# Moving two streamed activation tiles by 16 bytes within their partitions, in a kernel of three transformer layers

## The chip, the cores and the metric

The kernel runs on one core of one Trainium2 chip. The metric is the device time of one execution in microseconds (us); the kernel before has a median of 1132.21 us over 3 runs.

## The reference

Two blocks run one behind the other on 256 tokens of width 1024, all in float32. The first has two layers (a mixer and an MLP with squared ReLU each) and a final norm, the second has one layer. Cut to its core:

```python
for i in range(2):
    hn = rms_norm(x, norm_mix[i])
    mix = even_mixer(hn, ...) if i % 2 == 0 else odd_mixer(hn, ...)
    x = x + mix
    x = x + sqrelu_mlp(rms_norm(x, norm_mlp[i]), mlp_w1[i], mlp_w2[i])
x = rms_norm(x, norm_final)

h = rms_norm_2(x, mix_norm_pre)
xa, ga, q, k, v, f_logit, g_a, g_b = jnp.split(h @ w_in, offs, axis=-1)
y_a = gelu(ga) * rg_lru(causal_dwconv(xa, conv_a_w, conv_a_b), ...)
y_b = forgetting_attention(q, k, v, f_logit + b_forget)
merged = sigmoid(g_a + b_merge[0]) * (y_a @ w_proj_a) + sigmoid(g_b + b_merge[1]) * (y_b @ w_proj_b)
x = x + rms_norm_2(merged @ w_out, mix_norm_post)
h = rms_norm_2(x, ffn_norm_pre)
gate, val = jnp.split(causal_dwconv(h @ w_up, conv_f_w, conv_f_b), 2, axis=-1)
x = x + rms_norm_2((gelu(gate) * val) @ w_down, ffn_norm_post)
```

Here `even_mixer` holds a sparse attention with three branches and a differential attention, `odd_mixer` a block attention. Most of the arithmetic is products with the weight matrices, in float32, each read once.

## The kernel before

The activations lie transposed: 128 partitions hold a slice of the features, the 256 tokens lie along the partition. A tile of width 1024 is `[128, 8, 256]`, eight slices (`KT`, index k) of 256 float32 values, 1024 bytes each.

A float32 product is made of three matmuls of type `float32r`. Each operand is split into a high part and a low part, and `mm3` (lines 279 to 282) adds high x high, high x low and low x high in PSUM. The weights are the stationary operand, the activations the streamed one:

```python
def mm3(o, wh, wl, xh, xl, start, stop, skip=False):
    nc.tensor.matmul(out=o, lhsT=wh, rhs=xh, start=start, stop=False, skip_group_check=skip)
    nc.tensor.matmul(out=o, lhsT=wh, rhs=xl, start=False, stop=False, skip_group_check=skip)
    nc.tensor.matmul(out=o, lhsT=wl, rhs=xh, start=False, stop=stop, skip_group_check=skip)
```

`gh` and `gl` (lines 121 and 122) are the high and the low part of the normed layer input. Nearly all stages that read the residual stream take them as `xh` and `xl`: the projections into the mixers (lines 1168 on, 1290 on, 1512 on), the first matrix of both MLPs (`gen_pair(16, gh, gl, ...)` in `mlp`), the output projection of the second block (line 1635) and its up projection (line 1699). The second matrices of the MLPs stream `hh` and `hl`, the attention outputs `oh` and `ol`, the recurrent branch `yh` and `yl`. ACT and DVE write `gh` and `gl` between the stages (`split`, lines 269 to 277, and lines 1644 and 1648).

Three loops do the streaming with `mm3`: `gen_pair` (two units of weights of 128 columns per PSUM tile, eight k each), `gen_deep` (a matrix with 24 or 32 slices), `gen_half` (four slices at a time). `gen_small` does the same with weights of 24 or 16 columns. In `gen_nat` (lines 453 to 455) and `gen_wide` (lines 475 to 477) the roles are exchanged: the weight matrix is streamed, 256 or 512 columns of it, and a slice of `gh` or `gl` is the stationary operand.

Weights come as chunks of 1 MB into three buffers `raw` by DMA from the SP queue (`w_load`, line 198). `w_parts` splits half a chunk at a time into a unit: ACT copies it into `whi` (line 238), DVE subtracts to get `wlo` (line 239); six buffers of each hold the units for PE, and `w_next` (line 254) keeps three units ahead. The order on every engine is written out by hand (`tc.manual_schedule()`); the pieces of an attention are woven between the matmuls of the projections.

Where a tile lies in its partition is set by the order of the pools and by `pad`, which allocates a filler tile of n float32:

```python
pad(xp, 32)
x = xp.tile([128, KT, T], F32, name="x")
pad(xp, 48)
gh = xp.tile([128, KT, T], FR, name="gh")
gl = xp.tile([128, KT, T], FR, name="gl")
```

The pools stand in the order `cp`, `xp`, `np` (norms: `acc`, `rn`, `rv`, `dg`, `rb`, `sq`, `rb1`), `rawp` (`raw`, `raws`), `wp` (`whi`, `wlo`, behind `pad(wp, 96)` on line 190), and then the pools of the single stages, most of them behind a `pad` of 48. By this the streamed tiles `gh`, `gl`, `hh`, `hl`, `oh`, `ol`, `yh` and `yl` begin 192 bytes behind a multiple of 512, and `whi` and `wlo` at a multiple of 512. Tile starts are given by the pools in steps of 32 bytes.

Of the kernel before, what the change touches and what calls it, by code (L numbers as in the profile page):

```python
# [8 lines left out]
FR = mybir.dt.float32r  # L9
# [5 lines left out]
T = 256  # L15
D = 1024
KT = 8
# [41 lines left out]
def kernel(  # L59
# [30 lines left out]
    xp = ctx.enter_context(tc.tile_pool(name="xp", bufs=1))  # L90
# [3 lines left out]
    def pad(pool, n):  # L94
        pads.append(0)
        pool.tile([128, n], F32, tag="pad%d" % len(pads), name="pad", bufs=1)

    rawp = ctx.enter_context(tc.tile_pool(name="rawp", bufs=3))
    wp = ctx.enter_context(tc.tile_pool(name="wp", bufs=6))
# [18 lines left out]
    pad(xp, 32)  # L118
    x = xp.tile([128, KT, T], F32, name="x")
    pad(xp, 48)  # L120
    gh = xp.tile([128, KT, T], FR, name="gh")
    gl = xp.tile([128, KT, T], FR, name="gl")

    R_CMP, R_ATT0, R_ATT1, R_ATT2 = 2.0, 0.33, 0.7, 1.3

# [61 lines left out]
    add_stream(w_up, U8)  # L187
    add_stream(w_dn, U8)

    pad(wp, 96)  # L190
    W = Ctl()
    W.raw = []
    W.q = []
# [1774 lines left out]
```

## Time and profile before

| | |
|---|---|
| median of 3 runs | 1132.21 us |
| the runs | 1131.8, 1132.21, 1145.28 us |
| the profiled execution: its own time | 1144.74 us |
| its span, first to last instruction | 1143.0 us |
| mean granted TensorE clock | 0.993 |
| busy: PE, PEld, DVE, ACT, POOL | 97%, 93%, 67%, 54%, 18% |
| moved by DMA | 199.98 MB, mean 175 GB/s |

PE is the matrix engine's matmuls, PEld its weight loads (which overlap the matmuls), DVE the vector engine, ACT the scalar engine, POOL GpSimd, SP the engine whose queue issues the weight loads from memory. The profile is one execution; its own time exceeds its span by what lies before the first and behind the last instruction, 1.7 us. Matmuls overlap: the duration of one runs from its start until its last result, so two or three are in flight at a time, and the rate is read from starts or from counts over a stretch. PEclk is the granted clock as a share of 2.4 GHz.

### The profile page before, as it was taken

Reading aid. Unit: us, or ns where it says so; the run is one execution under the profiler, and the core shown is the slowest. Engines: PE = TensorE matmul, PEld = TensorE weight load, DVE = VectorE, ACT = ScalarE, POOL = GpSimd, SP = SyncE. Lnnn points to the kernel's source line nnn. Section 1 sums busy time; section 2 is a strip of 40 time slices with the busy share of each in tenths; the row PEclk is TensorE's granted clock in tenths of the full one; section 3 lists DMA queues with packets and bytes.
Section 4 is the critical chain, followed back from the end, with each engine's and each line's share of the span. In section 5 each row is a group of like instructions: output and inputs, shape, how many; then the busy total and the mean of one; then the engine's idle time right before and its main releaser. Section 6 shows DMA issues by size and latency. Waiting matters only on the chain.

```text
span 1143.0 us, 22253 instructions
## 1 busy us (share of the span) xinstructions
PE 1112.3 (97%) x9151; PEld 1062.5 (93%) x9151; DVE 768.0 (67%) x1355; ACT 615.2 (54%) x1081; POOL 204.4 (18%) x228
## 2 busy tenths in 40 slices
PE   8999899999999999999999999999999989999996
PEld 7987799999999898999999998899899989999996
DVE  5767776665445776666454688866667679988642
ACT  4446555654434555465353486754455557766441
POOL 2014420000010122000011100043310125444211
PEclk9999999999999999999999999999999989999998
DMA  8842243565454333455545454474455535555541
GB/s 329 297 149 74 75 163 139 214 217 197 179 221 177 121 122 146 144 214 185 221 151 227 177 196 147 149 271 140 147 193 174 184 130 171 201 190 188 193 148 37
DMA packets 31301, 199.98 MB, mean 175 GB/s; under 512 B 3594, under 2 KB 6042, under 8 KB 9056
## 3 DMA queue, kind: packets, MB, share of 16 engines
q1 hardware_dynamic: 28832, 187.23, 45.6%
q0 software_dynamic: 2080, 11.08, 2.9%
q8 instruction: 72, 1.18, 0.4%
q10 hardware_dynamic: 288, 0.26, 0.1%
q14 instruction: 29, 0.24, 0.1%
HBM read 197.43 MB, written 3.22 MB: 176 GB/s over the span
## 4 chain that ended last, share of the span: by engine, by line
PE 88%; DVE 5%; ACT 3%; POOL 1%; DMA 1%; issue 1%; SPq 0%; POOLq 0%; ACTq 0%; DVEq 0%
PE g L280 25%; PE g L282 24%; PE g L281 24%; PE rgp L1453 2%; PE pt L660 1%; PE g L475 1%; PE g L477 1%; PE g L476 1%; PE o L710 1%; PE s L616 1%; DVE wlo L239 1%; ACT whi L238 1%; DMA x<-in_xT_dram 1%; PE nsum L342 1%; DMA fb<-scr 1%
## 5 line engine op out<-in xcount | busy, mean ns | idle before, releaser
L239 DVE TENSOR_TENSOR wlo<-raw,whi 128x1024 fp32r<-128x1024 f32 (+2 forms) x356 | 427.8, 1232 | 120.8 <-ACT whi L238 120.5
L280 PE MATMUL g<-gh,whi 128*128 128x256 f32 x1632 | 463.3, 284 | 4.2 <-ACT whi L238 2.7
L281 PE MATMUL g<-gl,whi 128*128 128x256 f32 x1632 | 457.5, 280 | 0.5 <-DVE gl L275 0.4
L282 PE MATMUL g<-gh,wlo 128*128 128x256 f32 x1632 | 457.4, 280 | 0.3
L238 ACT CAST whi<-raw 128x1024 fp32r<-128x1024 f32 (+2 forms) x356 | 349.8, 1024 | 20.4 <-PE g L281 9.7
L280 PEld LDWEIGHTS g<-gh,whi 128*128 128x128 f32 x1632 | 309.7, 190 | 11.6 <-issue 4.8
L281 PEld LDWEIGHTS g<-gl,whi 128*128 128x128 f32 x1632 | 310.7, 190 | 1.2 <-DVE gl L275 0.7
L282 PEld LDWEIGHTS g<-gh,wlo 128*128 128x128 f32 x1632 | 309.9, 190 | 1.1 <-DVE wlo L239 1.1
L280 PE MATMUL g<-hh,whi 128*128 128x256 f32 x704 | 196.6, 279 | 0.0
L282 PE MATMUL g<-hh,wlo 128*128 128x256 f32 x704 | 196.5, 279 | 0.0
L281 PE MATMUL g<-hl,whi 128*128 128x256 f32 x704 | 196.5, 279 | 0.0
L282 PEld LDWEIGHTS g<-hh,wlo 128*128 128x128 f32 x704 | 133.3, 189 | 0.0
L281 PEld LDWEIGHTS g<-hl,whi 128*128 128x128 f32 x704 | 132.9, 189 | 0.0
L280 PEld LDWEIGHTS g<-hh,whi 128*128 128x128 f32 x704 | 132.2, 188 | 0.0
L335 POOL TENSOR_TENSOR acc<-acc,sq 128x256 f32<-128x256 f32 x53 | 42.3, 803 | 464.4 <-ACT sq L331 463.5
L649 POOL TENSOR_TENSOR p<-p,rr 128x384 f32<-128x384 f32 x56 | 50.2, 896 | 199.8 <-DVE rr L644 92.4
L634 ACT ACTIVATE p<-p,nm 128x256 f32<-128x256 f32 x112 | 49.9, 448 | 54.4 <-DVE nm L625 54.2
L280 PE MATMUL g<-oh,whi 128*128 128x256 f32 x192 | 54.9, 286 | 0.0
L1202 ACT ACTIVATE u<-u 128x512 f32<-128x512 f32 x32 | 20.2, 633 | 62.0 <-DVE u L1201 62.0
L281 PE MATMUL g<-ol,whi 128*128 128x256 f32 x192 | 53.5, 278 | 0.0
L282 PE MATMUL g<-oh,wlo 128*128 128x256 f32 x192 | 53.4, 278 | 0.0
L272 DVE TENSOR_TENSOR hl<-u,hh 128x512 fp32r<-128x512 f32 x32 | 22.2, 693 | 43.3 <-ACT hh L271 43.3
(320 smaller groups left out, 1388.5 us busy)
## 6 DMA issues: line engine op xcount, KB each, us to landing
raw<-in_w_in_dram SPq DMA_DIRECT2D x30, 1024.0 KB, 4.9
raw<-in_w_up_dram SPq DMA_DIRECT2D x24, 1024.0 KB, 4.8
raw<-in_w_m1a_dram SPq DMA_DIRECT2D x16, 1024.0 KB, 4.8
raw<-in_w_m2a_dram SPq DMA_DIRECT2D x16, 1024.0 KB, 4.9
raw<-in_w_m1b_dram SPq DMA_DIRECT2D x16, 1024.0 KB, 4.8
raw<-in_w_m2b_dram SPq DMA_DIRECT2D x16, 1024.0 KB, 4.9
raw<-in_w_od_dram SPq DMA_DIRECT2D x12, 1024.0 KB, 5.0
raw<-in_w_dn_dram SPq DMA_DIRECT2D x12, 1024.0 KB, 4.9
```

The costliest lines, as they stand in the source:

```text
L238: nc.scalar.copy(out=hi[:, a:b], in_=t[:, off + a:off + b])
L239: nc.vector.tensor_tensor(out=lo[:, a:b], in0=t[:, off + a:off + b], in1=hi[:, a:b].bitcast(F32), op=ALU.subtract)
L272: nc.vector.tensor_tensor(out=lo, in0=src, in1=hi.bitcast(F32), op=ALU.subtract)
L280: nc.tensor.matmul(out=o, lhsT=wh, rhs=xh, start=start, stop=False, skip_group_check=skip)
L281: nc.tensor.matmul(out=o, lhsT=wh, rhs=xl, start=False, stop=False, skip_group_check=skip)
L282: nc.tensor.matmul(out=o, lhsT=wl, rhs=xh, start=False, stop=stop, skip_group_check=skip)
L335: nc.gpsimd.tensor_tensor(out=self.acc, in0=self.acc, in1=dst, op=ALU.add)
L342: nc.tensor.matmul(out=ps[:, b:b + 1], lhsT=self.parts[i][:, b * 128:b * 128 + 128], rhs=ones[:, 0:1], start=i == 0 and b == 0, stop=i == ...
L634: nc.scalar.activation(out=p[:, c0:c1], in_=p[:, c0:c1], func=AF.Exp, scale=-1.0, bias=nm[:, b:b + 1], accum_out=sm[:, b:b + 1],)
L649: nc.gpsimd.tensor_tensor(out=pv, in0=pv, in1=w, op=ALU.mult)
L1202: nc.scalar.activation(out=u, in_=u, func=AF.Square)
L1453: nc.tensor.matmul(out=ps[c, m, :], lhsT=w[:, m, prs[pi], c], rhs=xc[:, half * 5 + pi, :], start=n == 0, stop=n == len(order) - 1, skip_gr ...
```

## The change

`gh` and `gl` become the two halves of one tile that is 8 float32 longer than both, and begin 4 float32 (16 bytes) into it. The filler before `whi` is made 8 float32 smaller.

```diff
     pad(xp, 48)
-    gh = xp.tile([128, KT, T], FR, name="gh")
-    gl = xp.tile([128, KT, T], FR, name="gl")
+    ghl = xp.tile([128, 2 * KT * T + 8], FR, name="gh")[:, 4:4 + 2 * KT * T].rearrange("p (a k t) -> p a k t", a=2, t=T)
+    gh, gl = ghl[:, 0], ghl[:, 1]
...
-    pad(wp, 96)
+    pad(wp, 88)
```

| tile | start behind a multiple of 512 before, bytes | after |
|---|---|---|
| `gh`, `gl` | 192 | 208 |
| `acc` | 192 | 224 |
| `dg`, `rb`, `sq` | 320 | 352 |
| `raw`, `raws` | 384 | 416 |
| `whi`, `wlo` | 0 | 0 |
| `hh`, `hl`, `oh`, `ol`, `yh`, `yl` | 192 | 192 |

The instructions of each engine, their order and the semaphores and values they wait for are the same in both programs; in the changed one both halves go by the name `gh`.

## Rows read from the trace of the kernel before

**Rows 1.** The page: busy us (share of the span), and the span in 40 slices

```profile
PE 1112.3 (97%) x9151; PEld 1062.5 (93%) x9151; DVE 768.0 (67%) x1355; ACT 615.2 (54%) x1081; POOL 204.4 (18%) x228
...
PE   8999899999999999999999999999999989999996
...
PEclk9999999999999999999999999999999989999998
```

**Rows 2.** The page's costliest groups: busy us, mean ns of one, idle before

```profile
L280 PE MATMUL g<-gh,whi 128*128 128x256 f32 x1632 | 463.3, 284 | 4.2 <-ACT whi L238 2.7
L281 PE MATMUL g<-gl,whi 128*128 128x256 f32 x1632 | 457.5, 280 | 0.5 <-DVE gl L275 0.4
L282 PE MATMUL g<-gh,wlo 128*128 128x256 f32 x1632 | 457.4, 280 | 0.3
```

**Rows 3.** Table of stretches (us): busy and count by engine, clock, DMA share, GB/s

```profile
187.00:242.00 55.00, 55.00 (x488) 55.00 (x487) 38.88 (x43) 31.89 (x41) 0.00 (x0) 1.00 0.55 195
250.00:325.00 75.00, 75.00 (x664) 75.00 (x663) 39.91 (x44) 33.34 (x44) 4.44 (x6) 1.00 0.52 197
473.50:534.00 60.50, 60.50 (x516) 60.50 (x515) 41.72 (x46) 35.34 (x46) 0.00 (x0) 1.00 0.57 200
545.00:620.00 75.00, 75.00 (x639) 75.00 (x638) 34.99 (x39) 32.18 (x47) 8.42 (x12) 1.00 0.50 192
945.00:1056.00 111.00, 111.00 (x944) 111.00 (x944) 102.57 (x146) 77.73 (x125) 50.93 (x43) 1.00 0.54 183
1062.00:1124.00 62.00, 62.00 (x529) 62.00 (x528) 28.01 (x27) 26.66 (x39) 8.51 (x10) 1.00 0.41 146
```

**Rows 4.** Timeline of PE at 182 us: start us, duration us

```profile
182.03 0.28 PE L281 MATMUL g<-gl,whi 128*128 128x256 f32 x1
182.46 0.39 PE L282 MATMUL g<-gh,wlo 128*128 128x256 f32 x1
182.68 0.28 PE L280 MATMUL g<-gh,whi 128*128 128x256 f32 x1
```

**Rows 5.** Timeline of PE at 473 us

```profile
472.73 0.28 PE L281 MATMUL g<-gl,whi 128*128 128x256 f32 x1
473.15 0.38 PE L282 MATMUL g<-gh,wlo 128*128 128x256 f32 x1
473.37 0.28 PE L280 MATMUL g<-gh,whi 128*128 128x256 f32 x1
```

**Rows 6.** Groups of PE by line and shape, 701 to 702.5 us

```profile
L280 PE MATMUL gs<-gh,whi 128*16 128x256 f32 x5 | 1.4, 276 | 0.0
L281 PE MATMUL gs<-gl,whi 128*16 128x256 f32 x5 | 1.4, 276 | 0.0
L282 PE MATMUL gs<-gh,wlo 128*16 128x256 f32 x5 | 1.4, 276 | 0.0
```

**Rows 7.** The same view, gen_nat, 67.5 to 69.5 us, then 70.5 to 72.5 us

```profile
L453 PE MATMUL g<-whi,gh 128*128 128x256 f32 x7 | 1.9, 276 | 0.0
...
L453 PE MATMUL g<-whi,gh 128*128 128x256 f32 x6 | 1.7, 279 | 0.0
```

**Rows 8.** The same view, 187 to 242 us, then 473.5 to 534 us

```profile
L281 PE MATMUL g<-gl,whi 128*128 128x256 f32 x163 | 45.0, 276 | 0.0
...
L281 PE MATMUL g<-gl,whi 128*128 128x256 f32 x172 | 48.3, 281 | 0.0
```

**Rows 9.** The page: splitting of weights on DVE and ACT, and loads of weights

```profile
L239 DVE TENSOR_TENSOR wlo<-raw,whi 128x1024 fp32r<-128x1024 f32 (+2 forms) x356 | 427.8, 1232 | 120.8 <-ACT whi L238 120.5
...
L238 ACT CAST whi<-raw 128x1024 fp32r<-128x1024 f32 (+2 forms) x356 | 349.8, 1024 | 20.4 <-PE g L281 9.7
...
raw<-in_w_in_dram SPq DMA_DIRECT2D x30, 1024.0 KB, 4.9
```

**Rows 10.** The page: the chain that ended last, by line

```profile
PE g L280 25%; PE g L282 24%; PE g L281 24%; PE rgp L1453 2%; PE pt L660 1%; PE g L475 1%; PE g L477 1%; PE g L476 1%; PE o L710 1%; PE s L616 1%; DVE wlo L239 1%; ACT whi L238 1%; DMA x<-in_xT_dram 1%; PE nsum L342 1%; DMA fb<-scr 1%
```

## The prediction

> **What bounds the kernel now.** I read the page's busy shares first, then the costliest groups of instructions, then the table of stretches, and last the timeline at two places where the matrix engine stood still.
>
> The busy shares and the slices [rows 1] show one bound: PE is busy 97% of the span, its slices are full from the first to the last, its clock is at the upper of its two levels (2.4 GHz) nearly throughout, and DVE and ACT stand at 67% and 54%. The costliest groups [rows 2] say what PE does: the three matmuls of `mm3`, lines 280 to 282, 1632 of each with `gh` or `gl` streamed. The change shifts just this streamed operand. Their printed mean of 280 ns is the life of one matmul, which overlaps its neighbours; what counts is the distance from one start to the next. That distance is read from the stretches [rows 3]: width divided by count, after taking off about 2 matmuls that are still in flight at the left edge.
>
> - 187 to 242 us, `gh` streamed, first feed-forward block: 55.0 / 486 = 113.2 ns
> - 250 to 325 us, `hh` streamed, same block: 75.0 / 662 = 113.3 ns
> - 473.5 to 534 us, `gh`, second feed-forward block: 60.5 / 514 = 117.7 ns
> - 545 to 620 us, `hh`, same block: 75.0 / 637 = 117.7 ns
> - 945 to 1056 us, `gh`, and 1062 to 1124 us, `hh`, last block: 111.0 / 942 = 117.8 and 62.0 / 527 = 117.6 ns
>
> So the same instruction on the same addresses runs at two spacings, 113.3 and 117.7 ns, 4.4 ns apart, at a granted clock of 1.00 in all six stretches. It doesn't go by the other engines (DVE is busy 39 of 55 us in the first stretch and 35 of 75 us in the fourth) nor by DMA (195 and 192 GB/s). A spacing holds for hundreds of matmuls and passes from `gh` to `hh` without a break. The timeline shows where it is chosen [rows 4, 5]: at 182.0 and at 472.7 us the next L282 starts 0.43 and 0.42 us after the matmul before it, the one behind follows after 0.22 us, and then a spacing settles: the short one that the first stretch shows behind the first place, the long one that the third shows behind the second. Nothing in the instructions tells the two places apart, so I take it to be the moment of restart.
>
> Two more groups bound what the operands' start has to do with it. With weights of only 16 columns, `gh` streamed, the spacing is still the short one [rows 6]: 1.5 us hold 15 less 2, 115 ns with the coarse edge. So 113.3 ns is the streaming alone, not the weight load. In `gen_nat` the roles are exchanged: `whi` and `wlo`, which begin at a multiple of 512, are streamed and `gh` is the weight. Both lives appear there too [rows 7], 276 ns (the short spacing's, as in the first stretch of [rows 8]) and 279 to 280 ns (the long one's is 281, second stretch). So starts of 0 and of 192 behind a multiple of 512 give the same two spacings.
>
> **The change part by part.** No instruction, wait or DMA is added, removed or moved; the terms are durations alone.
>
> 1. Streaming `gh` and `gl` from 208 instead of 192: 3 x 1632 matmuls [rows 2] and 48 in `gen_small`, 4944 in all. No row shows a streamed start that is no multiple of 64 with this type, so I bound it. 256 columns at 2.4 GHz would take 106.7 ns; the short spacing is 113.3 ns, 272 cycles: 16 more than the columns. The 1024 bytes are 16 pieces of 64, so one extra cycle per piece fits; a start at 208 cuts them into 17 pieces, one cycle or 0.42 ns more: 4944 x 0.42 = 2.1 us. Lower end: the whole surcharge of 6.7 ns vanishes, 4944 x -6.7 = -33 us. Upper end: if the reader takes 32 bytes at a time, 33 pieces in place of 32 cost 113.3 / 32 = 3.5 ns, +17.5 us. The two ends are far apart. The nearest rows are those of starts 0 and 192, which agree with each other (a cost of nothing), so I take the small value, +2.1 us.
> 2. `gh` and `gl` as weights, in the 144 matmuls of `gen_nat` and 192 of `gen_wide`: the load of 128 columns lies beside streaming; even 4.4 ns on each is 1.5 us. I take 0, range 0 to +1.5.
> 3. ACT and DVE writing `gh` and `gl`: a few hundred instructions off the bound, 0.
> 4. The tiles between `gl` and `whi` (`acc`, `rn`, `rv`, `dg`, `rb`, `sq`, `rb1`, `raw`, `raws`) move by 32 bytes; `whi`, `wlo` and all behind them stay. The 1 MB loads into `raw` land in 4.9 us [rows 9] while the DMA share of the big stretches is 0.41 to 0.57 [rows 3], so half of the queue's time covers them. L238 and L239 read `raw` in 1024 and 1232 ns [rows 9]. If they slowed by one part in sixteen, as streaming does against its ideal, the idle third of DVE and half of ACT hide it. The chain that ended last holds them for 1% of the span each [rows 10], some 23 us, so 1.5 us would show. I take 0, range 0 to +1.5.
>
> The sum: +2.1 us on the profiled execution of 1144.7 us gives 1146.8 us. That execution isn't like the median: 1131.8 and 1132.2 us stand against 1145.3 us, two levels 13 us apart, and the profile is on the upper one. The four stretches at the long spacing [rows 3] hold 514 + 637 + 942 + 527 = 2620 matmuls; at the short one they would save 2620 x 4.4 = 11.5 us, nearly that distance. So I read the median as an execution in which these two blocks fell on the short side (an estimate; no trace of such a run is at hand). Median plus the same term: 1132.2 + 2.1 = 1134.3 us.
>
> Here a rule speaks against any effect. The Trainium skill, SBUF — State Buffer, section "Who interferes with whom", gives PE two read ports and says that PE and ACT never wait on anyone; its section on Door 1 puts lines at 16 bytes, which 208 respects as well as 192. By both the sum is 0 and the time 1132.2 us. The trace bears out the second (starts of 0 and 192 agree) but not the first: equal instructions at 113 and 118 ns [rows 3] mean that something in PE's reading waits. The Trainium skill, TensorE: Matmul & The Clock Gate, section "Back-to-back issue gap", has N/2.4 + 2.5 ns, 109.2 ns for 256 columns; none of the stretches reaches it, and the measured spacings are used.
>
> **The rivals.**
>
> *The shift locks `gh` into the long spacing.* With weights at multiples of 512 and the stream 16 bytes off, the two reads may meet at every start; the rate is then set in `gh` and carried into `hh`, as it is at 242 and 535 us now. For it: the long spacing exists, is carried over, and lasts. Against it: in [rows 7] the relative start is the opposite and the choice is the same. Price from the median as read above: of the 4944 the 486 + 514 + 942 of the stretches run short there, and of the other 3002 I take half (both spacings occur in the stages with attention, as in [rows 7]), 3443 x 4.4 = 15.1 us, or 1147.3 us. With the 662 + 637 + 527 that follow in `hh` come 8.0 more, 1155.3 us. So it passes 2% (1154.9 us, 22.6 us above the median) where the carry-over is complete, or where the 17.5 us of term 1 (1149.7 us) come with some blocks at the long spacing.
>
> *The shift frees `gh` of the long spacing.* Then the profiled execution loses the 4.4 ns on 514 + 942 of the long stretches, on half of the other 3002, and on the 637 + 527 of `hh` that follow: 4121 x 4.4 = 18.1 us, 1126.6 us. From the median, whose long blocks are short already, the half of 3002 is left, 6.6 us: 1125.6 us. For it: a new phase between stream and weights is what the shift makes. Against it: the restarts decide now, and they stay.
>
> *Nothing in the rate moves, but the restarts fall otherwise.* The blocks fall on either side per execution; a median on the upper level is 1145 us with a change of nothing. Speaks for it: half of the four executions shown are there.
>
> *The surcharge goes:* 1132.2 - 33 = 1099 us. Against it: the 113.3 ns stand at both starts seen.
>
> **How the numbers follow.** Forecast (rates as now, at most a cycle per matmul, median on the lower level): 0.46. Restarts otherwise, 1138 to 1147 us: 0.16. Locked long or a dearer start: 0.22, of which 0.10 past 2%. Freed: 0.12. Surcharge gone: 0.04. 2% is about what a measurement of this kernel can tell from no change. Slower by over 2% is 0.10, faster by over 2% is 0.04, the same 0.86. The range runs from the freed case less some, 1123 us, to the complete lock, 1158 us; the forecast's own range, without the upper level, is 1130 to 1139 us.
>
> **What would show it.** In the changed kernel's stretches of `gh` I expect 113.7 ns where a block falls short (272 + 1 cycles) and about 118 ns where long, with `hh` still at 113.3 or 117.7, restarts still deciding, and no step at the border of `gh` and `hh` beyond 0.4 ns. The lock shows as every `gh` stretch at 118 ns or more; the freeing as every one at 113; a dearer start as a spacing near 117 with lives that differ from `hh`. The prediction is wrong if `gh` matmuls show a third spacing, below 112 or above 119 ns, or if ACT and DVE durations on `raw` move.

## The result and the profile after

The changed kernel has a median of 1152.31 us over 4 runs (1151.03 to 1153.6 us). Beside it the kernel before has 1138.74 us over 4 runs (1131.8 to 1145.41 us). The ratio is 1.0137, 95% interval 1.0094 to 1.018: slower by 1.4%. The forecast of 1134.3 us was 18 us low; its range, 1123 to 1158 us, holds the result, but the forecast's own range within it, 1130 to 1139 us, doesn't.

The page of the changed kernel first: busy times, PE's slices and its clock, the costliest groups of PE with `gh` and with `hh` streamed (busy us, mean ns of one, idle before), the splitting of the weights and one of the weight loads.

```profile
PE 1121.7 (97%) x9151; PEld 1071.0 (93%) x9151; DVE 770.4 (67%) x1355; ACT 615.3 (53%) x1081; POOL 211.0 (18%) x228
...
PE   8999899999999999999999999999999989999996
...
PEclk8999999999999999999999999999999989999998
...
L239 DVE TENSOR_TENSOR wlo<-raw,whi 128x1024 fp32r<-128x1024 f32 (+2 forms) x356 | 427.3, 1231 | 121.8 <-ACT whi L238 121.5
L280 PE MATMUL g<-gh,whi 128*128 128x256 f32 x1632 | 467.7, 287 | 4.0 <-ACT whi L238 2.5
L281 PE MATMUL g<-gh,whi 128*128 128x256 f32 x1632 | 462.1, 283 | 0.5 <-DVE gh L275 0.4
L282 PE MATMUL g<-gh,wlo 128*128 128x256 f32 x1632 | 461.8, 283 | 0.2 <-DVE wlo L239 0.2
L238 ACT CAST whi<-raw 128x1024 fp32r<-128x1024 f32 (+2 forms) x356 | 349.7, 1023 | 17.8 <-PE g L281 9.5
...
L281 PE MATMUL g<-hl,whi 128*128 128x256 f32 x704 | 195.2, 277 | 0.0
...
raw<-in_w_in_dram SPq DMA_DIRECT2D x30, 1024.0 KB, 4.9
```

The bound is the one of [rows 1]: PE 97%. The three groups of `gh` live 287, 283 and 283 ns where [rows 2] has 284, 280 and 280. L238, L239 and the loads into `raw`, whose tiles moved by 32 bytes, stand at 1023 and 1231 ns and 4.9 us, as in [rows 9].

Where the time went shows in the table of stretches (width, PE busy and count, granted clock, DMA share, GB/s). It answers to [rows 3]; the `hh` stretches begin a little later, because `gh` ends later.

```profile
187.00:242.00 55.00, 55.00 (x464) 1.00 0.58 205
251.00:325.00 74.00, 74.00 (x655) 1.00 0.55 206
473.50:534.00 60.50, 60.50 (x510) 1.00 0.49 175
547.00:620.00 73.00, 73.00 (x647) 1.00 0.53 201
945.00:1056.00 111.00, 111.00 (x953) 1.00 0.56 190
1071.00:1124.00 53.00, 53.00 (x452) 1.00 0.47 167
```

Two matmuls in flight taken off, as in the prediction:

- `gh`: 55.0 / 462 = 119.0 ns, 60.5 / 508 = 119.1 ns, 111.0 / 951 = 116.7 ns
- `hh`: 74.0 / 653 = 113.3 ns, 73.0 / 645 = 113.2 ns, 53.0 / 450 = 117.8 ns

So the first `gh` stretch, 113.2 ns before, is at 119.0, and `gh` doesn't reach the short spacing in any stretch. `hh` still shows both spacings. At the border of `gh` and `hh` in the first MLP this makes a step of 5.7 ns, with no wait between them; the prediction had allowed 0.4 ns.

The distances from start to start, summed over all matmuls of one streamed operand, account for the two profiled executions. `gh` and `gl` took 594.6 us before and 606.6 us after (+12.0), `hh` and `hl` 246.1 and 242.5 (-3.6), `oh` and `ol` 70.5 and 69.7 (-0.8). That is +7.6 us (the smaller groups nearly cancel), and the spans differ by 1150.6 - 1143.0 = 7.6 us. Of the 12.0 us, 1.2 are matmuls of `gen_small` at the lower clock (last section). The 7.6 us are less than the difference of the medians, 13.6 us, because the profiled execution of before was one of its long ones (1144.74 us). After the change the runs lie within 2.6 us of each other; before they spread over 13.6 us.

One place shows what does not cost. `gen_small` streams the same `gh` against weights of 16 columns. Groups of PE by line and shape in the changed kernel, 707 to 710 us:

```profile
L280 PE MATMUL gs<-gh,whi 128*16 128x256 f32 x8 | 2.2, 278 | 0.0
L282 PE MATMUL gs<-gh,wlo 128*16 128x256 f32 x8 | 2.2, 276 | 0.0
L281 PE MATMUL gs<-gh,whi 128*16 128x256 f32 x8 | 2.2, 276 | 0.0
```

A life of 276 ns is the short spacing's [rows 6, 8], and 2.5 us from 707.4 us on hold 24 matmuls. So streaming from 208 is as quick here as from 192, and the start alone doesn't make the 119 ns. The weights beside it differ in two ways: 16 columns instead of 128, and slices that begin 64 bytes apart instead of 512. These rows don't tell which of the two counts.

### The profile page after: what moved, and what is told of

It reads as the page before. It is cut to its first block, busy times and chain, and to the rows that moved or that the text cites. A ratio compares the mean times of both kernels' runs of the same rounds, so it can differ in the third digit from the quotient of the medians.

```text
span 1150.6 us, 22253 instructions
## 1 busy us (share of the span) xinstructions
PE 1121.7 (97%) x9151; PEld 1071.0 (93%) x9151; DVE 770.4 (67%) x1355; ACT 615.3 (53%) x1081; POOL 211.0 (18%) x228
## 4 chain that ended last, share of the span: by engine, by line
PE 89%; DVE 4%; ACT 3%; POOL 2%; DMA 1%; issue 1%; SPq 0%; POOLq 0%; ACTq 0%; DVEq 0%
PE g L280 25%; PE g L281 25%; PE g L282 24%; PE rgp L1453 2%; PE g L475 1%; PE pt L660 1%; PE g L477 1%; PE g L476 1%; PE o L710 1%; ACT whi L238 1%; PE s L616 1%; DVE wlo L239 1%; POOL acc L335 1%; DVE gh L275 1%; PE nsum L342 1%
## 5 line engine op out<-in xcount | busy, mean ns | idle before, releaser
L239 DVE TENSOR_TENSOR wlo<-raw,whi 128x1024 fp32r<-128x1024 f32 (+2 forms) x356 | 427.3, 1231 | 121.8 <-ACT whi L238 121.5
L280 PE MATMUL g<-gh,whi 128*128 128x256 f32 x1632 | 467.7, 287 | 4.0 <-ACT whi L238 2.5
L281 PE MATMUL g<-gh,whi 128*128 128x256 f32 x1632 | 462.1, 283 | 0.5 <-DVE gh L275 0.4
L238 ACT CAST whi<-raw 128x1024 fp32r<-128x1024 f32 (+2 forms) x356 | 349.7, 1023 | 17.8 <-PE g L281 9.5
L280 PEld LDWEIGHTS g<-gh,whi 128*128 128x128 f32 x1632 | 310.5, 190 | 11.6 <-issue 5.5
L281 PEld LDWEIGHTS g<-gh,whi 128*128 128x128 f32 x1632 | 310.5, 190 | 1.2 <-DVE gh L275 0.7
```

What stands on the lines that cost most here:

```text
L238: nc.scalar.copy(out=hi[:, a:b], in_=t[:, off + a:off + b])
L239: nc.vector.tensor_tensor(out=lo[:, a:b], in0=t[:, off + a:off + b], in1=hi[:, a:b].bitcast(F32), op=ALU.subtract)
```

## The experiments

Starts below are bytes behind a multiple of 512; "difference" is the start of the streamed tile less that of `whi`, modulo 512. Kernels called all-16, all-48 and all-8 put every streamed tile at the difference of 192. Ratios are to the kernel before, run beside each kernel on the same chip. Its medians there were 1137.1, 1137.96, 1137.12 and 1138.45 us, with runs from 1128.06 to 1145.74 us.

**1. The neighbours alone.** From the changed kernel, `gh` goes back to 192, the longer tile and the shifted `acc` ... `raws` stay.

```diff
-...name="gh")[:, 4:4 + 2 * KT * T]...
+...name="gh")[:, 0:0 + 2 * KT * T]...
```

> gh and gl are one longer tile again, but begin at its first element, 192 bytes behind a multiple of 512; acc, rb, sq, raw and the rest move by 32 bytes as in the changed kernel. Pair theory (the start of the stream against the start of the weights sets the spacing) and single theory (the start of the stream alone sets it): the time of the kernel before, 1132 to 1146 us, gh at 113.3 or 117.7 ns from start to start. Neighbour theory (the 32-byte move of the other tiles is what costs): 1150 to 1154 us, gh near 119 ns.

Measured: 1136.03 us (1129.73 to 1144.19, 10 runs), ratio 0.9974 (0.9935 to 1.0012). The table of stretches of its profile:

```profile
187.00:242.00 55.00, 55.00 (x488) 1.00 0.58 204
251.00:325.00 74.00, 74.00 (x655) 1.00 0.54 200
473.50:534.00 60.50, 60.50 (x536) 1.00 0.58 206
547.00:620.00 73.00, 73.00 (x646) 1.00 0.52 197
945.00:1056.00 111.00, 111.00 (x945) 1.00 0.56 191
```

`gh` is back at 55.0 / 486 = 113.2, 113.3 and 117.7 ns, both spacings of before. The shifted neighbours show no cost (the interval of the ratio holds 1); the start of `gh` and `gl` is the cause.

**2. The weights moved too.** From the changed kernel, `whi` and `wlo` become slices of two long tiles and begin at 16. `gh` against the weights is again 192 apart, `hh`, `oh` and `yh` (still at 192) are 176 apart.

```diff
-    W = Ctl()
+    W, WB = Ctl(), [wp.tile([128, 6 * 1024 + 128], FR, name=n, bufs=1)[:, 4:4 + 6 * 1024] for n in ("whi", "wlo")]
...
-        hi = wp.tile([128, 1024], FR, tag="hi", name="whi")
-        lo = wp.tile([128, 1024], FR, tag="lo", name="wlo")
+        hi, lo = [t[:, W.n % 6 * 1024:W.n % 6 * 1024 + 1024] for t in WB]
```

> gh and gl at 208 as in the changed kernel, and whi and wlo begin 16 bytes behind a multiple of 512 in place of 0, all six buffers of each. Pair theory: gh is back at 113.3 or 117.7 ns; hh, oh and yh, which stay at 192, are now the ones that are off by 16 and take about 119 ns; with 4944 matmuls of gh and 2928 of the others the time is about 1152 - 4944 x 4 + 2928 x 4 ns, some 1144 us (1138 to 1150). Single theory: gh stays near 119 ns, hh at 113.3 or 117.7, 1149 to 1154 us.

Measured: 1142.34 us (1141.61 to 1143.16, 10 runs), ratio 1.0057 (1.0022 to 1.0092). Its table of stretches:

```profile
187.00:242.00 55.00, 55.00 (x488) 1.00 0.56 194
251.00:325.00 74.00, 74.00 (x625) 1.00 0.53 199
473.50:534.00 60.50, 60.37 (x532) 1.00 0.54 190
547.00:620.00 73.00, 73.00 (x617) 1.00 0.53 202
945.00:1056.00 111.00, 111.00 (x982) 1.00 0.58 197
1071.00:1124.00 53.00, 53.00 (x449) 1.00 0.35 124
```

The picture is turned round. `gh` at 208 is short everywhere (111.0 / 980 = 113.3 ns, where before had 117.8), and `hh`, whose address is the one of before, is at 74.0 / 623 = 118.8 and 73.0 / 615 = 118.7 ns. The start of the stream by itself doesn't decide; its place against the weights does.

**3. Other starts of `gh`, weights at 0.** The first two change the slice of the longer tile, the others the fillers.

```diff
-...name="gh")[:, 4:4 + 2 * KT * T]...
+...name="gh")[:, 8:8 + 2 * KT * T]...    (224; 2:2 for 200)
...
-    pad(xp, 48)
+    pad(xp, 64)    (256; 32 for 128, 128 for 0, 80 for 320; slice 0:0, pad(wp, ...) less by as much)
```

> gh and gl at 224, 32 bytes behind 192 and half of 64; nothing else differs from the changed kernel. If pieces of 32 bytes count: spacings and time of the kernel before, 1132 to 1146 us. If pieces of 64 count: gh never at 113.3 ns, 1150 us or more. Neighbour theory: as the changed kernel, 1150 to 1154 us.

> gh and gl at 200, 8 bytes behind 192. If pieces of 16 bytes count in the stream, 200 is worse than 208, over 1154 us. If only the distance to a multiple of 64 (or 32) in the pair counts, gh is again kept from 113.3 ns with a spacing of its own, 1145 to 1154 us. Neighbour theory: 1150 to 1154 us.

> gh and gl at 256 behind a multiple of 512, 64 further than before; weights at 0, the others at 192. If a difference that is a multiple of 64 is what lets the pair lock: gh at 113.3 or 117.7 ns and 1129 to 1146 us. If the difference must be 192 itself (a step of 128 or more): gh kept from 113.3 ns, 1145 us or more.

> gh and gl at 128, weights at 0, the others at 192. By now 192 and the exchanged pair of gen_nat lock, and 176, 200, 208, 224 and 256 don't. If the difference must be a multiple of 64 other than 256: gh at 113.3 or 117.7 ns, 1128 to 1146 us. If it must be 64 short of 256 or 64 past it: gh kept from 113.3 ns, 1148 to 1160 us.

> gh and gl at a multiple of 512, as the weights. Multiple of 64 other than 256: gh at 113.3 or 117.7 ns, 1128 to 1146 us. 64 short of 256 or past it only: gh kept from 113.3 ns, 1148 to 1160 us.

> gh and gl at 320, which is 64 past 256; gen_nat has that difference now, with weights at 192 and the stream at 0. Both theories: gh at 113.3 or 117.7 ns, 1128 to 1146 us. If which of the two operands leads matters, and 192 alone locks: 1148 to 1160 us.

| start of `gh` | median us (runs) | ratio (95%) | matmuls in 187 to 242 us and ns | in 473.5 to 534 us and ns |
|---|---|---|---|---|
| 224 | 1154.11 (4) | 1.012 (1.0081 to 1.0159) | 467, 118.3 | 513, 118.4 |
| 200 | 1167.38 (4) | 1.0241 (1.0202 to 1.0279) | 461, 119.8 | 506, 120.0 |
| 256 | 1156.56 (4) | 1.0198 (1.016 to 1.0237) | 461, 119.8 | 506, 120.0 |
| 128 | 1155.61 (2) | 1.0156 (1.0113 to 1.0199) | 466, 118.5 | 512, 118.6 |
| 0 | 1155.81 (2) | 1.0158 (1.0128 to 1.0187) | 460, 120.1 | 506, 120.0 |
| 320 | 1152.05 (2) | 1.0125 (1.0093 to 1.0156) | 469, 117.8 | 516, 117.7 |

Every one of them is slower than before, and none of these stretches has `gh` at 113.3 ns. I had taken multiples of 64 to be the good starts; 0, 128 and 256 refute that. At 320 the time falls where "192 alone locks" put it, but the trace isn't so clean. Its long stretches are at 117.7 to 118 ns, and yet two groups of 47 matmuls of `gh`, each behind a pause, run at 113.3 ns from start to start (62.92 to 68.13 us and 412.71 to 417.92 us), as do three shorter ones. Groups of PE by line and shape in that kernel, 413 to 417.7 us, show the short spacing's life:

```profile
L282 PE MATMUL g<-gh,wlo 128*128 128x256 f32 x15 | 4.1, 276 | 0.0
L280 PE MATMUL g<-gh,whi 128*128 128x256 f32 x15 | 4.1, 276 | 0.0
L281 PE MATMUL g<-gh,whi 128*128 128x256 f32 x14 | 3.9, 276 | 0.0
```

So of the differences tried (0, 128, 176, 192, 200, 208, 224, 256, 320) two give the short spacing with weights of 128 columns: 192 and, seldom, 320, which is 192 the other way round. At the others no kept trace has nine matmuls of `mm3` in a row at it. `gen_nat` agrees: its difference is 320 in the kernel before, where it has twice 23 distances in a row at 113 to 115 ns, and 192 in the kernel with `gh` at 320, where it has 21 and 9 in a row; in the changed kernel and with `gh` at 224, 200, 256, 128 and 0 it has none.

The start 200 has a cost of its own in `gen_small`. Groups of its `gen_small`, 716 to 718.5 us:

```profile
L280 PE MATMUL gs<-gh,whi 128*16 128x256 f32 x8 | 2.3, 282 | 0.0
L281 PE MATMUL gs<-gh,whi 128*16 128x256 f32 x8 | 2.2, 278 | 0.0
L282 PE MATMUL gs<-gh,wlo 128*16 128x256 f32 x7 | 2.0, 281 | 0.0
```

With 16 columns of weights it lives 278 to 282 ns, and 2.5 us hold 23. From start to start in the timeline this `gen_small` has 113.3 to 113.5 ns at 0, 192, 208 and 256, and 116.6 to 118.5 ns at 128, 200, 224 and 320. So some starts of `gh` cost something there too, but 208 isn't one of them. That the kernel at 200 takes 11 us more than the one at 256 has another ground: their `gh` stretches are alike (119.8 and 120.0 ns), but `hh`, whose address is the same in both, is long throughout behind `gh` at 200. By the distances from start to start it takes 249.3 against 240.2 us, and the spans differ by 8.6 us.

**4. Everything moved together.** To part the difference from the absolute place, all streams and the weights move by the same amount: 32 bytes by one filler in the kernel before (weights 32, streams 224), 16 bytes by longer tiles (weights 16, streams 208), 48 bytes (weights 48, streams 240), 8 bytes (weights 8, streams 200). The last three have the same allocations but for one filler; only the slices differ.

```diff
-    pad(xp, 48)
+    pad(xp, 56)    (weights 32, in the kernel before)
...
-    hh = hp.tile([128, 32, T], FR, name="hh")
-    hl = hp.tile([128, 32, T], FR, name="hl")
+    hhhl = hp.tile([128, 2 * 32 * T + 8], FR, name="hh")[:, 4:4 + 2 * 32 * T].rearrange("p (a k t) -> p a k t", a=2, t=T)
+    hh, hl = hhhl[:, 0], hhhl[:, 1]
...
(likewise oh and ol, yh and yl, with gh and whi as in experiment 2: weights 16; with pad(xp, 56): 48; with slices from 2: 8)
```

> The filler before gh is 8 float32 larger and nothing else is changed, so that all tiles behind it, streamed and weights, move by 32 bytes: weights at 32, streams at 224. If only the difference of the two starts counts: the spacings and the spread of the kernel before, 1129 to 1146 us. If the place of the weights decides which spacing a restart finds: one level, near 1126 us (always short) or near 1150 us (always long). If 224 is a dear start by itself: over 1150 us with gh at 118.3 ns as in the run with gh alone at 224.

> Everything of the pair moved by 16: whi and wlo at 16, and gh, gl, hh, hl, oh, ol, yh, yl all at 208 behind a multiple of 512. Pair theory with the weights at 16 always choosing the short spacing, as gh did in the run before: all of them at 113.3 ns, time 1142.3 less 2928 x 5.4 ns, 1126.5 us (1124 to 1130), with little spread. Pair theory alone (both spacings open again to every block): 1129 to 1146 us, spread over both levels. Single theory (a start of 208 costs by itself): over 1155 us.

> As e6, but weights at 48 and all streamed tiles at 240 behind a multiple of 512: 32 bytes further each, the same difference of 192. Theory (the place matters by whether it is an odd multiple of 16): the restarts always find the short spacing, all big stretches near 113.3 ns, 1128 to 1130 us with a narrow spread. Rival (only the place 16 does it, or e6's gain came from the longer tiles' layout): both spacings occur, 113.3 and 117.7 ns by stretch, 1130 to 1145 us with a median near 1137 us.

> As e6, but weights at 8 and all streamed tiles at 200 behind a multiple of 512: 8 bytes less each, the same difference of 192 and the same allocations. If the tile layout of e6 (weights in one long tile) made its gain, this stays at 1128 to 1130 us. If a start off the steps of 16 costs something of its own, as e4_gh_200 showed with 200/0 (118 to 123 ns), every big stretch lies at or above 116 ns and the time is 1155 us or more. If only the difference and the parity of 16 matter, both spacings occur and the median is near 1137 us.

| weights, streams | median us (lowest to highest, runs) | ratio (95%) |
|---|---|---|
| 32, 224 | 1137.22 (1130.09 to 1140.87, 10) | 0.9998 (0.9965 to 1.0031) |
| 16, 208 | 1128.79 (1128.24 to 1129.47, 12) | 0.9939 (0.9919 to 0.9958) |
| 48, 240 | 1128.95 (1127.55 to 1129.9, 7) | 0.991 (0.9881 to 0.9939) |
| 8, 200 | 1180.09 (1179.16 to 1180.93, 4) | 1.0362 (1.0307 to 1.0418) |

The table of stretches with weights at 16:

```profile
187.00:242.00 55.00, 55.00 (x488) 1.00 0.56 194
251.00:325.00 74.00, 74.00 (x655) 1.00 0.53 200
473.50:534.00 60.50, 60.50 (x536) 1.00 0.58 202
547.00:620.00 73.00, 73.00 (x647) 1.00 0.53 198
945.00:1056.00 111.00, 111.00 (x982) 1.00 0.59 200
```

and with weights at 8:

```profile
187.00:242.00 55.00, 55.00 (x458) 1.00 0.56 196
251.00:325.00 74.00, 74.00 (x615) 1.00 0.51 186
473.50:534.00 60.50, 60.41 (x500) 1.00 0.49 175
547.00:620.00 73.00, 73.00 (x606) 1.00 0.48 182
```

At 16 every stretch has 113.2 to 113.3 ns, `gh` and `hh` alike, and the profile at 48 has the same counts in these five stretches. At 8 they have 120.6 to 121.5 ns. At 32 the runs spread much as those of before do. So 192 between the starts is needed but isn't enough. With weights at 0 or 32 the restarts choose between both spacings; at 16 and 48 they come out short; at 8 never.

The kept traces show this choice. Take series of at least nine matmuls of `mm3` with all distances at 112 to 114 ns (short) or at 117 to 119 ns (long). From one series to the next the spacing switches 34 times in the kernel before, 33 times in experiment 1 and 32 times with weights at 32, and each time a pause or a matmul of another kind lies between. With weights at 16 and at 48 it never switches, over 59 and 61 such breaks. `gen_nat` goes the other way there: with its stream at 16 or 48 and its weights 192 further it has one short series, of 9 or 10 distances, where the kernel before has two of 23; that costs 0.2 us.

The kernel at 16 and the one at 48 beat both kernels of this case, and do so by removing the spread: all their runs lie at 1127.55 to 1129.9 us, where only 4 of the 59 runs of before lie. That it isn't the longer tiles that help is shown by 8, which has them too.

The spacings also add up. In the all-16 kernel the matmuls of `gh` follow each other at 113.74 ns (mean of the distances under 130 ns, so without pauses); in the changed kernel it is 118.47 ns. Over 4944 matmuls this is 23.4 us, but pauses take up some of it: with them the distances of `gh` sum to 586.1 and 606.6 us, 20.5 us more. `hh`, in part long in the changed kernel, adds 2.4 us and `gen_wide` 0.9 us. Together that is 23.8 us, and the two spans differ by 23.7 us. In experiment 2 the same sums are 11.5 us (`hh`), 2.5 us (`oh`) and 0.7 us (`yh`) above those of all-16, and `gh` is 0.8 us below, mostly because its `gen_small` didn't meet the lower clock (last section); that is 13.9 us, and the spans differ by 14.1 us.

## Why the prediction was right or wrong

**The bound held.** PE is the bound before and after, the time moves with the spacing of its matmuls, and nothing else that was moved shows (term 4: L238, L239 and the loads unchanged; experiment 1: 0.9974 with 1 in its interval). Term 2 stays within its bounds: the 144 matmuls of `gen_nat` took 17.6 us from start to start before and after, the 192 of `gen_wide` 44.6 and 45.1 us.

**Term 1 is the step that failed.** It put +0.42 ns on a `gh` matmul, 2.1 us in all, from the nearest rows, "those of starts 0 and 192, which agree with each other". Measured are 118.47 ns against a mean of 115.6 in the profile of before and 113.74 in the all-16 kernel: +2.9 or +4.7 ns by what it is compared with. In the sums of all distances of `gh` this is 12.0 and 20.5 us. Two things were wrong in it. It looked for a cost of the stream alone, and that is nothing at 208, as `gen_small` shows (276 ns as before) and experiment 2, where `gh` at 208 runs at 113.3 ns beside weights at 16. And the rows of starts 0 and 192 [rows 7] were rows of `gen_nat`, in which the roles are exchanged: the stream is at 0 and the weights at 192. I read them as a statement on one start, when what counts is the pair: they agree because the two starts lie 192 apart in both. `gen_nat` itself shows it: its first 23 distances are 113 to 115 ns before, and 115 to 118 (the first one 120) in the changed kernel, where only its weights have moved. The upper bound of the term, +17.5 us, was about the right size for a wrong reason: it priced pieces of 32 bytes in the stream alone.

**"Nothing in the instructions tells the two places apart, so I take it to be the moment of restart"** holds for the kernel before, as its 34 switches show. The restarts choose between two spacings when the starts lie 192 apart and the weights stand at 0 or 32. At the other differences the short one isn't there to be chosen (at 320 it seldom is), and with weights at 16 or 48 the long one is not. Moving one tile by 16 bytes took the choice away, which the argument against the freed case ("the restarts decide now, and they stay") overlooked in both directions.

**The rival that locks `gh`** was right in place and sign and near in price: "the two reads may meet at every start", 1147.3 us for `gh` alone. Two of its parts were off. The rate isn't the long spacing of before but two new ones, 119.2 ns from start to start within the MLPs (past the 119 that the prediction had named as its refutation) and 116.7 ns in the up projection, in the mean 118.47, 4.7 ns over the short one where the rival had 4.4. And it isn't carried into `hh` as a rule: behind both MLPs' `gh` stretches `hh` runs at 113.3 and 113.2 ns, so 5.7 of the 8.0 us of the carry-over didn't come; in the last block `hh` is at 117.8 ns, where the profile of before has it too. The gap between 1147.3 us and the 1152.3 us measured lies mostly in its base and count: it took 1132.2 us with 1501 of 4944 matmuls already long, where the all-16 kernel, with all of them short, has 1128.8 us. The argument against it, [rows 7], is the misread pair again. A case that changes the pair of addresses of nearly all the matmuls should have had more weight than the 0.22 it got.

**The rule that PE never waits.** The Trainium skill, SBUF — State Buffer, section "Who interferes with whom", has it that PE and ACT never wait on anyone, and by it the sum was 0. These runs don't bear it out between PE's own two reads: the same matmul and the same weight load go from 113.3 to 119 ns by their starts alone. By the 16-byte lines that the Trainium skill gives on the same page, in its section on Door 1, 208 should have cost nothing either. They fit one thing only: the pair of 8 and 200, both off the steps of 16, is the slowest of all, 120.6 to 121.5 ns in the stretches. `gh` at 200 with weights at 0 isn't set apart by them, since 0 and 256 give the same 119.8 to 120.1 ns.

**The base of the forecast.** I read 1132.2 us as before's lower level with two blocks short. In four later sets its median was 1137 to 1138.5 us, and its lowest run 1128.06 us, so three runs had shown neither the middle nor the floor. By the same step, taken from its own base (1138.74 us), the forecast would have been 1140.8 us, still 11.5 us low.

**The range was luck.** It holds 1152.3 us because its upper end, 1158 us, was drawn to cover the complete lock; the case that was forecast, with 0.46, ended at 1139 us. The 0.86 for less than 2% came true in the same way, with the locking rival's smaller effect and not with the forecast's 2.1 us.

**What stays open.** No run shows what in the memory or in the reading makes 192 between the starts good, nor why 16 and 48 hold the short spacing while 0 and 32 allow both and `gen_nat` does the reverse. Why the pair of 208 and 0 runs at 119.2 ns in the MLPs and at 116.7 ns in the up projection is open as well. With `gh` at 200 and weights at 0, `hh` too was long throughout (117.6 to 117.9 ns), behind `gh` at 208 it was so only in the last block; which spacing `hh` takes behind a slow `gh` is not explained. Other differences than those named weren't tried.

## What to carry to other kernels

Where TensorE is the bound and every matmul loads new weights, look at the start-to-start distance by stretch, not at the busy share: two spacings of one instruction can come from the two operands' places. Then move both operands together before moving one, because here it was the distance between their starts (192), and the place of the pair (16 or 48 against 0, 32 or 8), that made 1128.8 or 1180 us of the same instructions. A tile that is moved by a few bytes has to be judged against each tile that is read at the same time, and a kernel whose runs spread over 1% without a cause is worth the same look.

## What was not expected of the hardware

- A shift of both operands by 16 bytes takes the spread out of the runs: 1.2 us over 12 runs, against 16 us (1128.06 to 1144.19) over the 23 runs of before beside them.
- A step of 8 bytes of everything, with nothing else changed, costs 1180.09 - 1128.79 = 51 us, 4.5%.
- In the profiled executions of the changed kernel and of the all-16 kernel (and of those with `gh` at 320 and with weights at 8), the granted clock went to the lower level (1.2 GHz) for some 3 us near 23 us, after a stretch of small matmuls of `nsum` and `gen_small`. There the matmuls of `gen_small` follow each other at 213 to 214 ns instead of 113. The profile of before has no such stretch there, so 1.2 us of its distance to the changed kernel are this; all-16 has it too and is the fastest.
